# In the couples of the down projection the fifth block product is put ahead of the seventh, and the split of the third pair's gate weights is recorded in VectorE's fixed order

## The chip, the cores and the metric

The kernel runs on one core of a Trainium2 chip. The metric is the time of one execution on the device in microseconds, taken as the median of several runs. The kernel before took 1000.0 us (three runs: 999.8, 1000.0 and 1000.95).

## The reference

One layer of an encoder block on x of 1024 positions by 1024 channels, in float32. What matters here is its second half, the gated MLP, and the fact that everything is a chain of large matrix products:

```python
        y = jnp.concatenate([y_a, y_b], axis=-1)
        x = x + jnp.einsum("bse,ed->bsd", y, w_out[l])

        h = rmsnorm(x, norm_ffn_g[l])
        g = dwconv(jnp.einsum("bsd,df->bsf", h, w_gate[l]), conv_ffn_w[l])
        v = jnp.einsum("bsd,df->bsf", h, w_up[l])
        x = x + jnp.einsum("bsf,fd->bsd", jax.nn.silu(g) * v, w_down[l])

    return rmsnorm(x, norm_final_g)
```

`w_gate` and `w_up` are 1024 x 2816, `w_down` is 2816 x 1024. The first half (two mixing branches and `w_out`) is touched by nothing in this change.

## The kernel before, in words

**Precision.** Every float32 operand is split into a high part, rounded to the matmul's reduced format by a ScalarE copy (L131), and a low part, the difference, made by a VectorE or GpSimd subtraction (L93). A product of two such operands is three matmuls: high by high, high by low, low by high. In the profile `whi` and `wlo` are the parts of a weight, `r` is a part of an activation block or of a weight that lies in the same arena.

**Seven products instead of eight.** The MLP's matrices are taken two by two blocks at a time and multiplied by Strassen's scheme in Winograd's form. `class Pair` (L546 on) has the seven block products, each a method that issues its matmuls through `mul` (L557, so all of them carry that line) and then an `after...` method that takes the result out of PSUM:

- `m1` = A11 by B11, which opens bank `a`; `m6` = S2 by T2, `m7` = S3 by T3 and `m4` = A22 by T4 go on adding into the same bank `a`. After each of the four the bank is read once, so every next product into `a` waits until the reading after the last one is done.
- `m2` = A12 by B21 in a bank `b` of its own.
- `m5` = S1 by T1, which opens bank `c`; `m3` = S4 by B22 goes on in it.

A and S are weight blocks: A11 and A12 are split from the raw weights `raw`, A22 from the second raw weights `up` (split into `ahi` and `alo`). S1 and S2 are sums that GpSimd makes (L511, tile `s`) and that are then split by ScalarE and VectorE into `whi` and `wlo`; S3 and S4 are made later from the same tile `s` and, in the down projection, are split into the arena tile `r_99`. B and T are activation blocks.

**Gate and up.** For each of 22 column blocks `f`, gate and up are one `Ffn` pair of weights. Blocks 0 and 1 are multiplied without the scheme (`Plain`); blocks 2 to 21 with it. `g_job(f)` (L481) loads the gate weights of block `f` and splits them, `ff_prep(f)` (L728) calls it, then loads the up weights and makes the sums. The blocks 0 to 2 start in a section in which the order on TensorE and VectorE is fixed as recorded (`tc.manual_schedule(engines={nc.tensor.engine, V.engine})`); from block 3 on, in the loop that follows, only TensorE's order is fixed and a list scheduler places what the other engines do. The activations of the MLP go to DRAM as blocks B11, T2, B21, T3, T1, T4 and B22.

**Down.** `w_down` is multiplied in three chunks `ch` of six column blocks, plus a tail of four blocks without the scheme. A `Down` object is one pair of output row blocks; two of them make a couple, and there are six couples (0 to 5), two for each chunk. For each couple the loop at L950 records, on TensorE in this order: `m1` of both pairs; `m3` of the couple before; then the five steps of `STEPS` (L909), each for both pairs. One product is nine matmuls here, 18 for a couple. Inside this loop only TensorE's order is fixed. Around the products the scheduler places:

- the preparation of the next couple (`down_prep`): two loads of `raw` and `up` for each pair, the split of A11 and A12 (`wlo<-raw,whi`), the sums on GpSimd and their split (`wlo<-s,whi`), for which there are four pairs of buffers;
- `prep3`: the sums S3 and S4 and their split (`r_99<-s,r_99`), and the split of A22 (`alo<-up,ahi`);
- the readings. `after1` is a ScalarE copy and a GpSimd addition (L90). `after2`, `after4`, `after5` and `after3` are VectorE additions from PSUM into the output (L863, `xd<-xd,b` and the like). `after6` and `after7` are VectorE additions too, `xr<-xr,a`; only in couple 0 (`early`) they are a ScalarE copy (L542) and a GpSimd addition;
- in the second couple of a chunk, couples 1 and 3, the load of the next chunk's activation blocks (`load_op`, named in `STEPS` beside each product). A block is loaded once the product that read the old one is done, and each of its three parts is split on ScalarE and VectorE (`load_split`). B11, T2, B21, T3, T1, T4 and B22 lie one behind the other in the arena tiles `r_96`, `r_97`, `r_94`, `r_95`, `r_98` and `r_99`: T3 fills most of `r_94`, T1 most of `r_95`.

In the trace each engine takes its instructions in the order in which the program has them, and one that waits holds up those behind it on its engine.

The line that sets the order of the five steps is, before:

```python
    STEPS = (("m6", "T2"), ("m2", "B21"), ("m7", "T3"), ("m5", "T1"), ("m4", "T4"))
```

Of the kernel before, what the change touches and what calls it, by code (L numbers as in the profile page):

```python
# [27 lines left out]
NHEAD = 2  # L28
# [17 lines left out]
def block_kernel(ctx: ExitStack, tc, xT, win01, win, wout, wgate, wup, wdown, consts, outT):  # L46
# [75 lines left out]
    def hilo():  # L122
        return [wspl.tile([P, D], F32R, tag=t, name=t) for t in ("whi", "wlo")]

    def load_raw(p, tag, src, n=D):
        t = p.tile([P, n], F32, tag=tag, name=tag)
        nc.sync.dma_start(t, src)
        return t

    def split(y, hi, lo, lo_eng):  # L130
        nc.scalar.activation(hi, y, AF.Copy)  # L131
        minus(lo_eng, lo, y, f32(hi))
# [43 lines left out]
    def total_parts(a, eng):  # L176
        st = stp.tile([P, S], F32R, tag="st", name="st")
        hi, lo = st[:, :H], st[:, H:]
        nc.scalar.activation(hi, a, AF.Copy)
        minus(eng, lo, a, f32(hi))  # L180
        return hi, lo
# [299 lines left out]
    def g_job(f):  # L481
        raw = load_raw(wraw, "raw", wgate[f])
        hl = hilo()
        split(raw, *hl, nc.vector)
        return raw, hl
# [15 lines left out]
    def g_parts(hl, n):  # L501
        return {"A11": parts(hl, 0, n), "A12": parts(hl, n * P, n)}
# [222 lines left out]
    def raw_u(f):  # L725
        return load_raw(rup, "up", wup[f])

    def ff_prep(f):  # L728
        raw, hl = g_job(f)
        fp[f].w.update(g_parts(hl, 4))  # L730
        up, s = raw_u(f), Sums(4)
        fp[f].w.update(s.first(raw, up))
        fp[f].w.update(s.second(raw, up, a22p))
# [7 lines left out]
    with tc.manual_schedule(engines={nc.tensor.engine, V.engine}):  # L741
        with urgent():
            hl = total_parts(accs2[1], V)
# [41 lines left out]
        with urgent():  # L785
            to_op("T2", 0, 0)
        p2.w.update(s2.second(g2[0], up2))
        plain[1].second_b()
    ucp.release()

# [3 lines left out]
    with tc.manual_schedule(engines={nc.tensor.engine}):  # L794
        for p in plain:
            p.finish()
        for f in range(NHEAD, NF - 2):
            p, q = fp[f], fp[f + 1]
            ff_prep(f + 1)
            if f == NHEAD:  # L800
                p.m5()
                p.m6()
            else:
                p.m6()
                p.m5()
            q.m1()
            p.m7()
            q.m2()
            p.m4()
            p.m3()  # L810
# [5 lines left out]
    def xblock(o, k, z):  # L816
        return rblocks[OPS.index(o) * 2 * PPC + z * PPC + k]
# [5 lines left out]
    def load_op(ch, o):  # L823
        for k in range(PPC):
            load_split(xblock(o, k, 0), xblock(o, k, 1), yd[o][:, ch * PPC + k, :])
# [80 lines left out]
    def load_xd(d):  # L906
        nc.sync.dma_start(xf[d], x2d[d])

    STEPS = (("m6", "T2"), ("m2", "B21"), ("m7", "T3"), ("m5", "T1"), ("m4", "T4"))  # L909


    with tc.manual_schedule(engines={nc.tensor.engine}):
# [34 lines left out]
    with tc.manual_schedule(engines={nc.tensor.engine}):  # L947
        for d in range(3, KD):
            load_xd(d)
        for i, pair in enumerate(couples):  # L950
            ch = pair[0].ch
            reload = i % 2 and ch + 1 < NCH
            for p in pair:
                p.m1()
            if i:
                for p in couples[i - 1]:
                    p.m3()
            if reload:
                load_op(ch + 1, "B11")
            if ch and i % 2 == 0:  # L960
                load_op(ch, "B22")
            for p in pair:
                p.prep3()
            if i + 1 < len(couples):
                down_prep(i + 1)
            for step, o in STEPS:
                for p in pair:
                    getattr(p, step)()
                if reload:
                    load_op(ch + 1, o)  # L970


    free = rblocks[:16]
# [177 lines left out]
```

## Time and profile before

| what | value |
|---|---|
| median of three runs | 1000.0 us (999.8 to 1000.95) |
| the profiled execution | 1000.93 us |
| its span, first to last instruction | 999.1 us |
| mean granted TensorE clock | 0.993 |
| TensorE busy (4208 matmuls) | 967.5 us, 97% |
| VectorE busy (888 instructions) | 755.6 us, 76% |
| ScalarE busy (632) | 452.8 us, 45% |
| GpSimd busy (303) | 477.0 us, 48% |

The time of the profiled execution and its span differ by 1.8 us, which lies ahead of the first and behind the last instruction. The page of the profile lists busy time by engine and by group of instructions; the chain of waits follows the work that ended last back from the end; the timeline has instructions in order of time, with their start, their duration and, in brackets, the idle time of the engine just before them and who ended it. Engines are PE (TensorE), DVE (VectorE), ACT (ScalarE), POOL (GpSimd) and SP (the queue that issues loads and stores). A group such as `x18` is so many instructions one behind the other. The down section runs from about 759 to 934 us of the span, some 29 us for each couple.

### The profile page before, as it was taken

What the parts mean: (1) busy time and instruction counts of PE and PEld (TensorE: products, weight loads), DVE (VectorE), ACT (ScalarE), POOL (GpSimd) and SP (SyncE); (2) the same over time, 40 slices, a digit from 0 to 9 for tenths busy, and PEclk for the clock granted to TensorE, in tenths of its full rate; (3) what the DMA queues carried; (4) which work ended last, traced back from release to release, by engine and by line L of the source; (5) the groups of instructions that cost most, each with busy time, mean ns of one, the idle gap of its engine ahead of it and who ended that gap; (6) DMA issues with size and microseconds to landing.
All of it is one profiled execution on the core that took longest, in us unless ns stands there. A gap on an engine that the chain in (4) does not pass through costs nothing.

```text
span 999.1 us, 11602 instructions
## 1 busy us (share of the span) xinstructions
PE 967.5 (97%) x4208; PEld 790.8 (79%) x4208; DVE 755.6 (76%) x888; ACT 452.8 (45%) x632; POOL 477.0 (48%) x303
## 2 busy tenths in 40 slices
PE   7999999999999999999999999999998999999994
PEld 5788888888878887788888888888886787878883
DVE  7899999999578897855655565565569798796556
ACT  7454422234564456434444443444457263544353
POOL 4289754353853006554455456365336744352006
PEclk9999999999999999999999999999999999999998
DMA  6211111113554204143143133134284663643105
GB/s 257 85 44 63 43 45 61 42 64 106 193 190 153 76 0 158 64 148 106 64 145 108 64 124 129 64 101 141 70 287 130 220 207 96 194 127 109 61 1 169
DMA packets 63274, 112.56 MB, mean 113 GB/s; under 512 B 5488, under 2 KB 27120, under 8 KB 62960
## 3 DMA queue, kind: packets, MB, share of 16 engines
q1 hardware_dynamic: 62640, 110.65, 33.1%
q10 hardware_dynamic: 576, 1.17, 0.3%
q8 instruction: 33, 0.54, 0.2%
q14 instruction: 25, 0.20, 0.1%
HBM read 84.79 MB, written 27.00 MB: 112 GB/s over the span
## 4 chain that ended last, share of the span: by engine, by line
PE 81%; DVE 9%; ACT 3%; issue 2%; DMA 1%; POOL 1%; POOLq 0%; SPq 0%; DVEq 0%; ACTq 0%
PE a L557 30%; PE mm L166 20%; PE c L557 15%; PE b L557 7%; DVE r L93 2%; PE c L692 1%; PE a L692 1%; PE mm L153 1%; PE mm L152 1%; PE mm L154 1%; PE y L154 1%; PE y L152 1%; PE y L153 1%; DMA raw<-wgate 1%; ACT whi L131 1%
## 5 line engine op out<-in xcount | busy, mean ns | idle before, releaser
L166 PE MATMUL mm<-r,whi 128*128 128x512 f32 x576 | 155.8, 389 | 0.0
L557 PE MATMUL a<-r,whi 128*128 128x512 f32 x472 | 145.7, 390 | 0.4 <-ACT a L542 0.4
L323 DVE SCALAR_TENSOR_TENSOR cv<-u,cst,cv 128x512 f32<-128x512 f32 x203 | 138.9, 751 | 1.7 <-ACT cv L317 1.2
L511 POOL TENSOR_TENSOR s<-raw,s 128x512 f32<-128x512 f32 (+1 forms) x31 | 57.5, 1854 | 161.5 <-DVE wlo L93 161.5
L166 PEld LDWEIGHTS mm<-r,whi 128*128 128x128 f32 x576 | 108.1, 188 | 22.6
L557 PE MATMUL c<-r,whi 128*128 128x512 f32 x392 | 121.1, 390 | 0.0
L93 POOL TENSOR_TENSOR wlo<-raw,whi 128x1024 fp32r<-128x1024 f32 x30 | 77.5, 2586 | 88.0 <-ACT whi L131 88.0
L131 ACT ACTIVATE whi<-raw 128x1024 fp32r<-128x1024 f32 (+1 forms) x68 | 69.2, 1020 | 103.5 <-PE mm L166 32.0
L557 PEld LDWEIGHTS a<-r,whi 128*128 128x128 f32 x472 | 88.4, 188 | 19.7 <-ACT a L542 0.8
L511 POOL TENSOR_TENSOR s<-up 128x512 f32<-128x512 f32 (+1 forms) x31 | 42.0, 1354 | 116.7 <-DMA up<-wup 96.8
L557 PE MATMUL a<-r,wlo 128*128 128x512 f32 x236 | 92.2, 391 | 2.8 <-DVE wlo L93 2.8
L166 PE MATMUL mm<-r,wlo 128*128 128x512 f32 x288 | 90.0, 389 | 0.0
L557 PEld LDWEIGHTS c<-r,whi 128*128 128x128 f32 x392 | 73.8, 188 | 16.0
L542 ACT ACTIVATE a<-a 128x512 f32<-128x512 f32 x80 | 47.5, 595 | 66.9 <-PE a L557 64.2
L131 ACT ACTIVATE whi<-s 128x1024 fp32r<-128x1024 f32 (+1 forms) x52 | 52.5, 1010 | 53.5 <-PE c L557 39.8
L557 PE MATMUL c<-r,wlo 128*128 128x512 f32 x196 | 76.5, 390 | 0.0
L635 DVE TENSOR_TENSOR t<-a,c 128x512 f32<-128x512 f32 x40 | 27.5, 687 | 64.4 <-ACT a L542 38.1
L557 PE MATMUL a<-r,ahi 128*128 128x512 f32 x224 | 70.5, 396 | 1.4 <-ACT a L542 1.4
L557 PE MATMUL b<-r,whi 128*128 128x512 f32 x232 | 71.4, 389 | 0.0
L93 DVE TENSOR_TENSOR wlo<-s,whi 128x1024 fp32r<-128x1024 f32 (+1 forms) x52 | 64.2, 1236 | 5.8 <-ACT whi L131 5.7
L131 ACT ACTIVATE r<-r 128x512 fp32r<-128x512 f32 x71 | 43.8, 628 | 49.8 <-DMA r<-ydB 23.3
L166 PEld LDWEIGHTS mm<-r,wlo 128*128 128x128 f32 x288 | 54.1, 188 | 11.2
(214 smaller groups left out, 2142.0 us busy)
## 6 DMA issues: line engine op xcount, KB each, us to landing
raw<-wgate SPq DMA_DIRECT2D x22, 512.0 KB, 4.9
up<-wup SPq DMA_DIRECT2D x20, 512.0 KB, 3.6
raw<-win SPq DMA_DIRECT2D x18, 512.0 KB, 3.2
ydT<-t SPq DMA_DIRECT2D x36, 256.0 KB, 3.4
r<-ydT SPq DMA_DIRECT2D x36, 256.0 KB, 3.3
raw<-wout SPq DMA_DIRECT2D x16, 512.0 KB, 3.4
ydB<-t SPq DMA_DIRECT2D x27, 256.0 KB, 5.0
r<-ydB SPq DMA_DIRECT2D x27, 256.0 KB, 4.5
```

Source lines behind the costliest of these rows:

```text
L93: eng.tensor_tensor(out=out, in0=a, in1=b, op=ALU.subtract)
L131: nc.scalar.activation(hi, y, AF.Copy)
L152: nc.tensor.matmul(out, whi, hi, start=first, stop=False)
L153: nc.tensor.matmul(out, whi, lo, start=False, stop=False)
L154: nc.tensor.matmul(out, wlo, hi, start=False, stop=last)
L166: nc.tensor.matmul(outs[h], w, a[h][z], start=s0, stop=s1)
L323: nc.vector.scalar_tensor_tensor(fin if k == KC - 1 else acc, src, w, acc, ALU.mult, ALU.add)
L511: self.eng.tensor_tensor(out=self.t[:, i * self.w : (i + 1) * self.w], in0=a, in1=b, op=op)
L542: nc.scalar.activation(t, b, AF.Copy)
L557: nc.tensor.matmul(out, w[wz][:, k, :], x[xz], start=first and k + wz + xz == 0, stop=k == n - 1 and wz == 1, skip_group_check=not first)
L635: nc.vector.tensor_tensor(out=out, in0=a, in1=b, op=op)
L692: nc.tensor.matmul(out, w[wz][:, k, :], xz, start=first and k == 0 and wz == 0 and xz is hi, stop=not first and k == 3 and wz == 1)
```

## The change

It has two parts.

The first swaps two of the five steps of a couple. `m5` now comes before `m7`, and both loads that hung on `m7` and `m5`, T3 and T1, are recorded after `m7`:

```diff
-    STEPS = (("m6", "T2"), ("m2", "B21"), ("m7", "T3"), ("m5", "T1"), ("m4", "T4"))
+    STEPS = (("m6", ("T2",)), ("m2", ("B21",)), ("m5", ()), ("m7", ("T3", "T1")), ("m4", ("T4",)))
...
-            for step, o in STEPS:
+            for step, ops in STEPS:
                 for p in pair:
                     getattr(p, step)()
                 if reload:
-                    load_op(ch + 1, o)
+                    for o in ops:
+                        load_op(ch + 1, o)
```

The second takes the load and split of block 3's gate weights out of the loop and records it in the section before, in which VectorE's order is fixed, ahead of the last products of block 1:

```diff
-    def ff_prep(f):
-        raw, hl = g_job(f)
+    def ff_prep(f, job=None):
+        raw, hl = job or g_job(f)
...
         p2.w.update(s2.second(g2[0], up2))
+        job = g_job(NHEAD + 1)
         plain[1].second_b()
...
-            ff_prep(f + 1)
+            ff_prep(f + 1, job if f == NHEAD else None)
```

What this does to the order of the instructions, engine by engine: on all five engines the instructions, and what each waits for, are the same in both kernels from the start up to the middle of couple 0. The second part thus changes numbers of buffers, and moves nothing. On TensorE, in each of the six couples the 18 matmuls of `m5` now stand ahead of the 18 of `m7`; at the end, couple 5's `m4` stands some matmuls later among those of the tail.

VectorE in couple 1, before. The names ending in 5700 and 5701 are the outputs of the couple's two pairs; `a` is read after `m7`, `c` after `m5`; `r_94` and `r_97` are splits of reloaded blocks, `wlo<-s` is the split of S1 and S2 for couple 2:

```order
L93 TENSOR_TENSOR r_94<-r_94,r_97 128x512
L863 TENSOR_TENSOR xr_5700<-xr_5700,a 128x512
L93 TENSOR_TENSOR r_94<-r_94,r_97 128x512
L863 TENSOR_TENSOR xr_5701<-xr_5701,a 128x512
L93 TENSOR_TENSOR r_94<-r_94 128x512 x2
L863 TENSOR_TENSOR xr_5700<-xr_5700,c 128x512
L93 TENSOR_TENSOR wlo<-s,whi 128x768
L93 TENSOR_TENSOR r_94<-r_94 128x512
L863 TENSOR_TENSOR xr_5701<-xr_5701,c 128x512
L93 TENSOR_TENSOR wlo<-s,whi 128x768
```

The same place in the changed kernel, from the same split of `r_94` on:

```order
L93 TENSOR_TENSOR r_94<-r_94,r_97 128x512
L864 TENSOR_TENSOR xr_5700<-xr_5700,c 128x512
L93 TENSOR_TENSOR wlo<-s,whi 128x768
L93 TENSOR_TENSOR r_94<-r_94,r_97 128x512
L864 TENSOR_TENSOR xr_5701<-xr_5701,c 128x512
L93 TENSOR_TENSOR wlo<-s,whi 128x768
L93 TENSOR_TENSOR r_95<-r_95 128x512 x2
L864 TENSOR_TENSOR xr_5700<-xr_5700,a 128x512
L93 TENSOR_TENSOR r_95<-r_95 128x512
L864 TENSOR_TENSOR xr_5701<-xr_5701,a 128x512
L93 TENSOR_TENSOR r_94<-r_94 128x512 x3
```

The addition after `m7` of the couple's first pair (`xr_5700<-xr_5700,a`) now stands behind both additions of `c`, both splits of the next couple's sums and two splits of T1. Between the addition that comes before it on bank `a` (after `m6` of the second pair) and itself stood ten instructions; now there are seventeen: those ten and two additions of `c`, two splits `wlo<-s`, one more split of `r_94` and two of `r_95`. Couple 3 has the same seven.

ScalarE in couple 0, before. `a_5840` and `a_5852` are the copies of bank `a` after `m7` of the two pairs, `whi<-s` is the high part of couple 1's S1 and S2, `t` belongs to the last gate/up blocks:

```order
L131 ACTIVATE whi<-raw 128x768 x2
L542 ACTIVATE a_5840<-a 128x512
L613 ACTIVATE t<-t 128x1024
L542 ACTIVATE a_5852<-a 128x512
L131 ACTIVATE whi<-s 128x768 x2
L131 ACTIVATE ahi<-up 128x384 x2
```

And after, where the same two copies are called `a_5862` and `a_5874`:

```order
L131 ACTIVATE whi<-raw 128x768 x2
L131 ACTIVATE whi<-s 128x768
L613 ACTIVATE t<-t 128x1024
L131 ACTIVATE whi<-s 128x768
L542 ACTIVATE a_5862<-a 128x512
L542 ACTIVATE a_5874<-a 128x512
L131 ACTIVATE ahi<-up 128x384 x2
```

Both copies of bank `a` have moved behind both copies of the sums.

SP in couple 0, before. `xd_5699`, `xr_5700` and `xr_5701` are the output rows to which the products are added, `raw` and `up` are weights of couple 2:

```order
L616 DMA ytail<-t 128x1024 x2
L907 DMA xd_5699<-x2d 128x1024
L907 DMA xr_5700<-x2d 128x1024 x2
L907 DMA xr_5701<-x2d 128x1024 x2
L831 DMA raw<-wdown 128x3x128 x2
L831 DMA up<-wdown 128x3x128
```

And after:

```order
L616 DMA ytail<-t 128x1024 x2
L832 DMA raw<-wdown 128x3x128 x2
L908 DMA xd_5699<-x2d 128x1024
L908 DMA xr_5700<-x2d 128x1024 x2
L908 DMA xr_5701<-x2d 128x1024 x2
L832 DMA raw<-wdown 128x3x128 x2
```

Two loads of couple 2's raw weights, which wait until GpSimd has made couple 1's last sum from the same buffer, now stand ahead of the loads of the output rows.

## The prediction

> **What bounds the kernel now.** I read the page first. These lines are the span, TensorE's busy time and the shares of the chain of work that ended last:
>
> ```profile
> span 999.1 us, 11602 instructions
> PE 967.5 (97%) x4208; PEld 790.8 (79%) x4208; DVE 755.6 (76%) x888; ACT 452.8 (45%) x632; POOL 477.0 (48%) x303
> ...
> PE 81%; DVE 9%; ACT 3%; issue 2%; DMA 1%; POOL 1%; POOLq 0%; SPq 0%; DVEq 0%; ACTq 0%
> ```
>
> TensorE is busy for nearly the whole span and is 81% of the chain. So the kernel gets faster only where TensorE stands still, and slower where it is made to. The view of TensorE's waits names who was late, among others these (total us, times, longest):
>
> ```profile
> PE a L557 <- DVE r L93: 3.4, 2, 2.8
> ...
> PE a L557 <- DVE xd L863: 1.9, 2, 1.4
> ```
>
> Both concern products into bank `a`, which is where the change works. The chain of waits in order of time shows what a product costs in the down section. Its columns are start, duration, engine and line, count:
>
> ```profile
> 800.32 4.08 PE b L557 x18
> 804.40 4.08 PE a L557 x18
> 808.48 4.08 PE c L557 x18
> 812.56 8.31 PE a L557 x36
> ...
> 829.03 4.09 PE b L557 x18
> ...
> 834.52 4.35 PE a L557 x18
> ...
> 871.65 8.31 PE a L557 x36
> ...
> 888.12 2.05 PE b L557 x9
> ...
> 892.64 4.34 PE a L557 x18
> ```
>
> A product of a couple is 18 matmuls in 4.08 us, 0.227 us each. Couple 1 runs without a hole: second product at 800.32, seventh at 804.40, fifth at 808.48, fourth at 812.56. The x36 rows are the fourth product and the next couple's first. The other rows are the holes. In couple 2 the second product ends at 829.03 + 4.09 = 833.12, and the seventh starts at 834.52 and takes 4.35 instead of 4.08: 1.67 us lost. In couple 4 the second product has nine matmuls from 888.12 to 890.17, and nine more would end at 892.21; the seventh starts at 892.64 and takes 4.34: 0.69 lost. The large hole is in couple 0; these are TensorE's rows of its seventh product, up to the fifth:
>
> ```profile
> 769.98 0.61 PE L557 MATMUL a<-r,r 128*128 128x512 f32 x2
> 771.23 2.33 PE L557 MATMUL a<-r,r 128*128 128x512 f32 x9 [0.64 <-DVE r L93]
> 776.33 3.35 PE L557 MATMUL a<-r,r 128*128 128x512 f32 x7 [2.76 <-DVE r L93]
> 779.48 0.71 PE L557 MATMUL c<-r,whi 128*128 128x512 f32 x2
> ```
>
> The 18 matmuls take from 769.98 to 779.48, that is 9.50 us for work of 4.08: 5.42 lost. It waits for VectorE's splits of the sums S3, one for each pair:
>
> ```profile
> 769.13 2.05 DVE L93 TENSOR_TENSOR r<-s,r 128x768 fp32r<-128x768 f32 x1
> ...
> 774.26 2.01 DVE L93 TENSOR_TENSOR r<-s,r 128x768 fp32r<-128x768 f32 x1
> ```
>
> The seven matmuls from 776.33 to 779.48 are 3.15 us for work of 7 x 0.227 = 1.59, so 1.56 of the 5.42 is no wait but a slower clock. The view by windows shows that (width, busy times of PE, PEld, DVE, ACT and POOL, granted clock, DMA share and rate):
>
> ```profile
> 772.80:776.20 3.40, 0.77 (x4) 0.30 (x2) 3.40 (x3) 0.60 (x1) 3.40 (x3) 1.00 0.33 131
> 776.20:779.60 3.40, 3.27 (x8) 2.60 (x9) 3.40 (x4) 1.06 (x1) 3.32 (x3) 0.50 0.08 30
> ```
>
> **The second part of the change** moves no instruction, so TensorE's wait for that split, in the gate/up section, stays, and the part costs and brings nothing. The first row has the wait, the second what follows it; had the split moved, at most 1.8 us could go:
>
> ```profile
> 382.08 0.50 PE L557 MATMUL a<-r,wlo 128*128 128x512 f32 x1 [1.79 <-DVE wlo L93]
> 382.42 0.63 PE L557 MATMUL a<-r,whi 128*128 128x512 f32 x2
> ```
>
> **What the first part takes away.** With the fifth product in front, TensorE has 4.08 us of work from 769.98 to 774.06 that needs no S3. S1 and T1 are there: S1 is split together with S2, which the sixth product has already used, and T1's splits in couple 0 end long before. Then the first pair's seventh product needs the split that ended at 771.18, and the second pair's third matmul, due at 774.06 + 2.04 + 2 x 0.227 = 776.6, the one that ended at 776.27. The whole 5.42 goes. In couples 2 and 4 the wait is for the reading of bank `a` after the sixth product, late by less than 4.08, so it goes too. Together: 5.42 + 1.67 + 0.69 = 7.78 us.
>
> **What it brings: the fourth product comes straight behind the seventh.** Before, the fifth stood between them and gave the readers of bank `a` 4.08 us more. Now the first pair's fourth product is due when the second pair's seventh ends, 2.04 us after the first pair's. Who reads the bank, and what stands ahead of that reading, decides.
>
> Couple 0: the readers are ScalarE copies. Before, they ran when the seventh product was done. ScalarE's rows from the second of them on:
>
> ```profile
> 779.72 0.60 ACT L542 ACTIVATE a<-a 128x512 f32<-128x512 f32 x1 [0.35 <-PE a L557]
> 781.67 0.85 ACT L131 ACTIVATE whi<-s 128x768 fp32r<-128x768 f32 x1 [1.35 <-PE c L557]
> ```
>
> Now both copies stand behind both `whi<-s`, and the second of these needs GpSimd's sum of couple 1's second pair, in which nothing changes up to its end:
>
> ```profile
> 779.17 1.61 POOL L511 TENSOR_TENSOR s<-s,raw 128x384 f32<-128x384 f32 x1
> ```
>
> That sum ends at 780.78. The split's high part (0.85) then ends at about 781.7, and the copy (0.60) at 782.2. The seventh product ends at 778.14, so TensorE stands still for about 4.1 us. If GpSimd were a microsecond earlier it would be 3.1; 4.3 is the other end. Before, the fourth product started at 779.48 + 4.08 = 783.6, so couple 0 starts it only 1.3 earlier for all that was taken away.
>
> Couple 1: the reader is a VectorE addition, in a queue with no gaps. VectorE's rows, from the addition after the sixth product to the one after the seventh, and some behind it:
>
> ```profile
> 803.74 0.67 DVE L863 TENSOR_TENSOR xr<-xr,a 128x512 f32<-128x512 f32 x1
> 804.34 0.68 DVE L93 TENSOR_TENSOR r<-r 128x512 fp32r<-128x512 f32 x1
> 804.94 1.28 DVE L93 TENSOR_TENSOR r<-r,r 128x512 fp32r<-128x512 f32 x2
> ...
> 810.89 0.67 DVE L863 TENSOR_TENSOR xr<-xr,a 128x512 f32<-128x512 f32 x1
> ...
> 814.49 0.95 DVE L93 TENSOR_TENSOR wlo<-s,whi 128x768 fp32r<-128x768 f32 x1
> ...
> 816.55 1.18 DVE L93 TENSOR_TENSOR wlo<-s,whi 128x768 fp32r<-128x768 f32 x1
> 817.66 2.93 DVE L93 TENSOR_TENSOR r<-r 128x512 fp32r<-128x512 f32 x2
> ```
>
> From 804.34 to 810.89 lie ten instructions, eight of 512 columns at a step of 0.60 (804.34 to 804.94) and two of 768 columns, which leaves 0.87 for each. Now seven more stand ahead: two additions of `c`, one split of `r_94`, two of `r_95` (5 x 0.60) and two `wlo<-s` (2 x 0.87), 4.74 in all. The addition starts at 815.63 and ends at 816.30. The fourth product is due at 812.56 in either order, so it waits 3.7 us at the least. More is likely, since GpSimd makes its second sums as soon as the first `wlo<-s` is done:
>
> ```profile
> 815.51 1.40 POOL L511 TENSOR_TENSOR s<-raw,s 128x384 f32<-128x384 f32 x1 [12.24 <-DVE wlo L93]
> ...
> 820.00 1.47 POOL L511 TENSOR_TENSOR s<-raw,up 128x384 f32<-128x384 f32 x1
> ```
>
> They run for 6.0 us (815.51 to 821.47), and under them the second `wlo<-s` took 1.18 instead of 0.95 and two splits of `r_95` took 2.93 instead of 1.28. Before, that lay behind the addition. Now the first `wlo<-s` is the twelfth behind 804.34 and ends at about 804.34 + 9 x 0.60 + 3 x 0.87 = 812.4, so the sums fall on what lies ahead of the addition: 0.23 + 1.65 = 1.88 more, and the wait is 5.6 us. With the split of `r_94` slowed as well (0.8) it is 6.4. I take 5.6, since these are the same instructions under the same sums.
>
> Couple 3 has the same seven extra instructions:
>
> ```profile
> 860.40 1.27 DVE L863 TENSOR_TENSOR xr<-xr,a 128x512 f32<-128x512 f32 x2
> 861.60 2.71 DVE L93 TENSOR_TENSOR r<-r,r 128x512 fp32r<-128x512 f32 x2
> ...
> 868.97 0.68 DVE L863 TENSOR_TENSOR xr<-xr,a 128x512 f32<-128x512 f32 x1
> ```
>
> The addition goes from 868.97 to 873.71 and ends at 874.39; the fourth product is due at 871.65: 2.7 us, or 4.6 with GpSimd. Here two splits had already been slowed before (2.71 at 861.60), so not all is new. I take 3.6. Couples 2, 4 and 5 reload nothing: their queue holds only additions and the next splits, and the addition follows in time. I cost them at nothing; without that cover it would be some tenths each.
>
> The clock: one gap of 2.76 us cost 1.56 behind it, while behind the gap of 1.79 us at 382 two matmuls took 0.63, as two took 0.61 at 769.98, so the clock stayed full there. All three new gaps are longer than 2.76. I take the full 1.56 for the longest, and 1.0 for each of the others, since work may resume in the middle of a slow stretch: 3.6, with ends 0 and 4.7. The Trainium skill's "TensorE: Matmul & The Clock Gate", section "What's actually happening", says that the array falls to half rate only after a whole idle window of some 3.4 us, and that the windows run freely. By that rule a gap of 3.6 would hardly ever count and the longer ones only by luck of phase, so by it this term would be nearer to 1.5 and the sum 2 us less; the trace disagrees, with half rate behind 2.76 us.
>
> **What costs nothing else.** T1's reload starts 4 us earlier and T3's 4 us later, by the ends of their products, and each is needed only in the next couple's fifth or seventh, over 20 us on. The bank `c` opens 4 us earlier; its last user, two products of the couple before, is done by then. On SP two loads of raw weights now stand ahead of the output rows, and this addition waited for such a row already:
>
> ```profile
> 789.37 0.69 DVE L863 TENSOR_TENSOR xd<-xd,a 128x512 f32<-128x512 f32 x1 [1.91 <-DMA xd<-x2d]
> ```
>
> If the row comes 4 us later, the addition ends at 794. It is now the one after the fifth product, and the third product of that pair is due at about 794 as well. I take 0, with 1.0 as the upper end.
>
> **The sum.** -7.8 + 4.1 + 5.6 + 3.6 + 3.6 = +9.1 us. The profiled execution took 1000.93 (its span of 999.1 and 1.8 around it), so it would become 1010.0; it lies 0.9 above the median of the three runs, 1000.0, and on the median the forecast is 1009.1. The lower ends give -7.8 + 3.1 + 3.7 + 2.7 + 0 = +1.7, the upper ones -7.8 + 4.3 + 6.4 + 4.6 + 4.7 + 1.0 = +13.2.
>
> **The rivals.**
>
> *VectorE is in time (faster).* The place is the addition after the first pair's seventh product in couples 1 and 3. It turns where that addition ends before the fourth product is due, 812.56 in couple 1: seventeen instructions of 11.3 us and 0.67 must then start at 800.6, straight behind the sixth product, and not at 804.34. What speaks for it: in couple 3 the addition after the sixth product already came at 860.40, under 1 us behind the product (three products before 871.65 is 859.4). Against it: even there the new addition is 2.7 late. Only couple 0's gap and its clock would be left: -7.8 + 4.1 + 1.0 = -2.7, or 997.3.
>
> *The clock stays at full rate.* All three gaps come, and none is followed by a slow stretch: 9.1 - 3.6 = +5.5, 1005.5. For it speaks that the gap of 1.79 us left the clock alone; against it the 2.76. The Trainium skill's clock rule, above, is on this side.
>
> *Short queues.* GpSimd's sums fall elsewhere and the clock stays: -7.8 + 4.1 + 3.7 + 2.7 = +2.7, 1002.7.
>
> *Lateness is passed on.* The output rows hold up a third product and the queue in couples 2 and 4 is still late: 13.2 and some 2 more, 1015. Against it: each new gap of TensorE gives VectorE time to catch up.
>
> *The second part does what it says.* The wait of 1.8 us at 382 goes: 1007.3. The order speaks against it on every engine.
>
> **How the numbers follow.** Forecast, 1009.1 with a range of its own from 1006 to 1013.5: 0.68. Clock at full rate, 1005.5: 0.14. Short queues, 1002.7: 0.06. Passed on, 1015: 0.06. In time, 997.3: 0.05. Second part, 1007.3: 0.01. The range from 1003 to 1014 leaves out the short queues, the passed-on lateness and the rival in time, 0.17. A measurement of this kernel can tell 0.2%, or 2 us, from no change: below 998 lies the rival in time, 0.05; between 998 and 1002 the lower half of the short queues and what lies near, 0.04; above, 0.91.
>
> **What would show it.** In the profile after: TensorE's seventh product of couple 0 without a wait for VectorE's `r`, some 5 us gone; its fourth product in couple 0 waiting for ScalarE's copy (L542) for about 4 us, in couples 1 and 3 for VectorE's `xr` for about 5.6 and 3.6; the two holes in couples 2 and 4 gone; granted clock 0.50 behind the new gaps; the wait at 382 unchanged. I am wrong if the fourth product follows the seventh without a gap in couple 1, or if VectorE's addition there ends before 813.

## The result and the profile after

The changed kernel takes 1015.62 us (median of 4 runs, 1014.05 to 1016.75), the kernel before beside it 999.9 (999.42 to 1000.95): a ratio of 1.0155, 95% interval 1.0137 to 1.0172, 15.7 us slower. The forecast was 1009.1 with a range up to 1014.0. The sign and the places were as forecast, the size was not.

The profiled execution took 1016.0 us. Its span, TensorE's busy time and the shares of the chain of waits, from the page of the profile after:

```profile
span 1014.2 us, 11602 instructions
PE 972.8 (96%) x4208; PEld 795.6 (78%) x4208; DVE 754.4 (74%) x888; ACT 452.9 (45%) x632; POOL 473.0 (47%) x303
...
PE 74%; DVE 8%; issue 4%; ACT 4%; DMA 4%; POOL 3%; SPq 0%; POOLq 0%; ACTq 0%; DVEq 0%
```

The instructions are the same. TensorE's share of the chain fell from 81% to 74%, and DMA's rose from 1 to 4. TensorE's waits in the down section (758 to 940), total us, times and longest:

```profile
PE a L557 <- DVE xr L864: 11.5, 2, 7.4
PE a L557 <- ACT a L542: 4.1, 2, 3.9
PE a L557 <- DVE wlo L93: 0.7, 1, 0.7
```

The two waits of before, for VectorE's `r` and `xd`, are gone. In their place the fourth product waits for the readers of bank `a`. TensorE's rows in couples 0, 1 and 3, the seventh product (x18) and the first of the fourth:

```profile
773.65 4.24 PE L557 MATMUL a<-r,r 128*128 128x512 f32 x18
781.76 1.22 PE L557 MATMUL a<-r,ahi 128*128 128x512 f32 x2 [3.87 <-ACT a L542]
...
809.23 4.24 PE L557 MATMUL a<-r,r 128*128 128x512 f32 x18
820.89 1.22 PE L557 MATMUL a<-r,ahi 128*128 128x512 f32 x2 [7.42 <-DVE xr L864]
...
876.34 4.24 PE L557 MATMUL a<-r,r 128*128 128x512 f32 x18
884.62 1.22 PE L557 MATMUL a<-r,ahi 128*128 128x512 f32 x2 [4.04 <-DVE xr L864]
```

All three seventh products run through in 4.24 us, couple 0's too. From the start of the eighteenth matmul (0.227 us before the due time) to the next one it is 4.03, 7.58 and 4.20 us more than a step. And the clock behind each gap, by windows (width, busy times of PE, PEld, DVE, ACT and POOL, granted clock, DMA share and rate):

```profile
777.60:781.00 3.40, 0.29 (x2) 0.00 (x0) 3.40 (x4) 1.70 (x3) 2.67 (x2) 1.00 0.00 0
781.00:787.80 6.80, 6.04 (x14) 4.83 (x15) 6.24 (x7) 1.72 (x4) 5.09 (x4) 0.50 0.22 83
...
818.60:825.40 6.80, 4.51 (x11) 3.54 (x12) 5.71 (x9) 1.15 (x2) 2.50 (x2) 0.50 0.51 154
...
883.40:890.20 6.80, 5.58 (x13) 4.42 (x14) 5.63 (x9) 1.79 (x3) 1.43 (x2) 0.50 0.65 187
```

Before, one slow stretch of 3.4 us lay in this section. Now there are three of 6.8. In couple 0's fourth product three matmuls take 1.28 us at clock 0.50 (782.78 to 784.06) and 0.69 at full rate (788.11 to 788.80), so 0.46 of what lies between the first matmul and the end of the stretch is lost: 0.46 x (787.8 - 781.76) = 2.8 in couple 0, 0.46 x (825.4 - 820.89) = 2.1 in couple 1, 0.46 x (890.2 - 884.62) = 2.6 in couple 3, 7.4 together with the parts unrounded. With it the difference of the spans, 15.1 us, is told within 0.4 us: 4.03 + 7.58 + 4.20 + 7.4 - 7.78 = 15.4.

Where a kernel was run beside the kernel before on another chip, that took 1000.5 to 1000.8 there, and the ratios below are to it. They are worked out from the single runs, so they can differ a little from the quotient of the two medians.

### The profile page after: what moved, and what is told of

Read it like the earlier page. It is cut to its first block, busy times and chain, and to the rows that moved or that the text cites. A ratio compares the mean times of both kernels' runs of the same rounds, so it can differ in the third digit from the quotient of the medians.

```text
span 1014.2 us, 11602 instructions
## 1 busy us (share of the span) xinstructions
PE 972.8 (96%) x4208; PEld 795.6 (78%) x4208; DVE 754.4 (74%) x888; ACT 452.9 (45%) x632; POOL 473.0 (47%) x303
## 4 chain that ended last, share of the span: by engine, by line
PE 74%; DVE 8%; issue 4%; ACT 4%; DMA 4%; POOL 3%; SPq 0%; POOLq 0%; ACTq 0%; DVEq 0%
PE a L557 27%; PE mm L166 19%; PE c L557 13%; PE b L557 6%; DVE r L93 2%; POOL s L511 2%; PE c L692 1%; PE a L692 1%; DMA raw<-wout 1%; PE y L154 1%; PE y L152 1%; PE y L153 1%; ACT whi L131 1%; ACT r L131 1%; DMA r<-ydT 1%
## 5 line engine op out<-in xcount | busy, mean ns | idle before, releaser
L557 PE MATMUL a<-r,ahi 128*128 128x512 f32 x224 | 76.5, 425 | 16.0 <-DVE xr L864 11.5
L557 PEld LDWEIGHTS a<-r,ahi 128*128 128x128 f32 x224 | 45.6, 205 | 28.3 <-DVE xr L864 12.3
```

Source lines behind the costliest of these rows:

```text
L557: nc.tensor.matmul(out, w[wz][:, k, :], x[xz], start=first and k + wz + xz == 0, stop=k == n - 1 and wz == 1, skip_group_check=not first)
```

## Experiments: the parts one by one

The changed kernel with the new order of the steps in some couples alone (`i in (0,)`, `(1, 3)`, `(2, 4, 5)`), and one with the second part alone:

```diff
-            for step, ops in STEPS:
+            for step, ops in STEPS if i in (0,) else OLD:
```

> The changed kernel with the new order of the steps in couple 0 alone; the other five couples keep the old order. Theory (each couple adds its own part: in couple 0 the hole of 5.4 us ahead of the seventh product goes, a wait of 4.0 us ahead of the fourth product comes, and about 3.2 us of slow clock behind it): +1.8 us, 1001.7. Rival (my prediction's size of the clock term, 1.0 in this couple): -5.4 + 4.0 + 1.0 = -0.4, 999.5. Second rival (the lateness of couple 0 is what delays couple 1, in either order of couple 1): over 1003, with a wait in couple 1.

> The new order in couples 1 and 3 alone. Theory (nearly all of the loss is here: waits of 7.6 and 4.2 us ahead of the fourth product and 2.2 and 2.6 us of slow clock behind them): +16.6, 1016.5. If 1.2 us of couple 1's wait were inherited from couple 0, whose moved loads let the first splits of the reloaded block come late, couple 1's wait is 6.4 here, and the time 1015.3. Rival (my prediction: 5.6 and 3.6 us, clock 1.56 and 1.0): +11.8, 1011.7.

> The new order in couples 2, 4 and 5 alone, where nothing is reloaded. Theory (the holes of 1.67 and 0.69 us in couples 2 and 4 go, and the fourth product's wait stays covered): -2.4, 997.5. Rival (these queues are late as well as soon as couples 1 and 3 do not hold TensorE up): a wait ahead of the fourth product of some tenths to 2 us with slow clock behind it, 999 to 1002.

> Only the second part of the change: the split of block 3's gate weights recorded in the section with VectorE's fixed order, all couples in the old order. Theory (it moves no instruction): 999.9, and the wait of 1.8 us at 382 stays. Rival (it lets the split come in time): 998.1 without that wait.

| kernel | median us | ratio to before, 95% | difference by the ratio, us | forecast for this part |
|---|---|---|---|---|
| couple 0 | 1003.39 | 1.0026 (1.0015 to 1.0038) | +2.6 | -5.4 + 4.1 + 1.0 = -0.3 |
| couples 1 and 3 | 1014.04 | 1.0134 (1.0115 to 1.0153) | +13.4 | 5.6 + 3.6 + 2.6 = +11.8 |
| couples 2, 4 and 5 | 1000.93 | 1.0003 (0.9989 to 1.0017) | +0.3 | -2.4 |
| second part | 999.80 | 0.9997 (0.9986 to 1.0007) | -0.3 | 0 |

The four sum to 16.0, the whole has 15.5 by its ratio. Each of the first three came out 1.6 to 2.9 above its forecast, so no single term was wrong alone. That they add up so nearly is in part chance, since the parts act on each other, as the rows below show. The second part does nothing, as forecast.

Two rows say more. With the new order in couples 1 and 3 alone, couple 1 waits only 4.7 us, not 7.4:

```profile
818.67 1.22 PE L557 MATMUL a<-r,ahi 128*128 128x512 f32 x2 [4.68 <-DVE xr L864]
```

The rest of its wait is thus inherited from couple 0. Counted as above, couples 1 and 3 wait 4.8 and 4.6 us here, 9.4 together where the prediction had 9.2; the slow clock behind them takes 4.8 where it had 2.6. With the new order in couples 2, 4 and 5 alone, the hole of couple 2 only moves, from the seventh to the fourth product:

```profile
836.07 4.24 PE L557 MATMUL a<-r,r 128*128 128x512 f32 x18
842.47 0.73 PE L557 MATMUL a<-r,ahi 128*128 128x512 f32 x2 [2.16 <-DVE xd L864]
```

VectorE is still behind from couple 1's reload. In the whole change this wait does not come, because couple 1 has already held TensorE up for 7.4 us. The kernel with couples 1 and 3 alone bears that out: there too couple 2 has no wait for `xd`, although it keeps the old order.

## Experiments: the clock

To keep TensorE busy in the gaps without touching the waits, extra products go into a bank that nobody reads, in the changed kernel and in the one with couples 1 and 3:

```diff
+                if step == "m7" and i in FILL:
+                    z = bank2("z")
+                    for j in range(FILL[i]):
+                        pair[0].mul(z, "A22", "T4")
```

> The changed kernel with extra products in the three gaps: behind the seventh products of couples 0, 1 and 3 TensorE multiplies A22 by T4 into a bank that nobody reads, 18, 27 and 18 matmuls (4.1, 6.1 and 4.1 us at full rate), so that it is not idle while it waits for the readers of bank a. The waits themselves stay, covered by this work. Theory (the three slow stretches of 6.83 us come from the idle time ahead of them, and cost about 8.0 us together): 1015.6 - 8.0 = 1007.6, no clock of 0.50 in the down section; up to 1.5 less if the loads of couple 2's weights come earlier here and shorten couple 1's wait. My prediction's size of the clock term (3.6): 1012. Rival (the slow stretches do not come from idleness): 1015 or more, with 0.50 in the same places.

> The kernel with the new order in couples 1 and 3 alone (1014.0 us), with 18 extra matmuls (4.1 us, A22 by T4 into a bank that nobody reads) behind the seventh product of each of the two, where its waits of 4.8 and 4.6 us were followed by slow stretches. Theory (the slow clock comes from idleness, and here it lies on the path): no clock of 0.50 behind these two places and 2.45 + 2.7 = 5.1 us less, 1008.9. Rival (what TensorE wins by it, it loses at the next reading, since VectorE's queue and not TensorE sets the time here): no slow stretches either, but 1013 to 1014, with other waits longer by as much. Rival (the stretches do not come from idleness): 1014 with the 0.50 there.

The second (`FILL = {1: 2, 3: 2}`) took 1009.93 us, ratio 1.0094 (1.0079 to 1.0109), where the same order without the extra work has 1.0134 (1.0115 to 1.0153): 4.0 us less, of 5.1 expected. The clock by windows from the start of the fourth product in couples 1 and 3:

```profile
817.40:824.20 6.80, 6.80 (x30) 5.53 (x31) 5.80 (x10) 2.81 (x5) 0.17 (x1) 1.00 0.70 201
880.10:886.90 6.80, 6.80 (x30) 5.53 (x31) 5.96 (x11) 3.53 (x7) 0.06 (x1) 1.00 0.78 227
```

Thirty matmuls fit into 6.8 us, where the slow stretches of the change held eleven and thirteen and a rest of the gap. So the slow stretches come from the idle time, and in these two couples they are on the path.

The first (`{0: 2, 1: 3, 3: 2}`) took 1014.86, ratio 1.0140 (1.0120 to 1.0159), hardly less than the changed kernel: its expectation of 1007.6 failed. The slow stretches of couples 0 and 3 are gone, couple 1's of 6.8 us stays, and the time is not won. The chain of waits in order of time shows why:

```profile
786.90 0.38 SPq L832
...
787.87 5.93 DMA xd<-x2d
793.83 0.70 DVE xd L864
...
794.57 2.33 PE c L557 x9
```

Couple 0's third product now waits for the addition that read bank `c`, this for an output row, and that row stood on SP behind a load of raw weights. What couple 0 wins, it loses 10 us later at a row: its third product is due at 790.73 instead of 792.91, but the product behind it, couple 1's sixth, starts at 796.74, against 796.99 in the change. This is the move on SP that the prediction had priced at nothing. And what couple 3 wins by its clock is lost in couple 1, whose fourth product starts at 822.92 instead of 820.89, after a wait of 3.4 us: there the up weights had waited 3.9 us on SP for VectorE's split `alo` of the weights before them.

## Experiments: couple 1's wait

Four DMAs of couple 2's raw weights go to GpSimd's queue, where they stand behind GpSimd's own sum and hold up no load on SP; in another kernel the output rows go to ScalarE's queue; in a third GpSimd's second sums for couples 2 and 4 are left out:

```diff
-            nc.sync.dma_start(
+            (nc.gpsimd if tag == "raw" and ch == 1 and d < 4 else nc.sync).dma_start(
...
-        nc.sync.dma_start(xf[d], x2d[d])
+        nc.scalar.dma_start(xf[d], x2d[d])
...
+            if sums:
                 self.op(1, g[:, w : 2 * w], self.t[:, w : 2 * w], ALU.subtract)
                 self.op(0, g[:, :w], v[:, :w], ALU.subtract)
```

> The changed kernel with the loads of couple 2's raw weights, four DMAs, issued by GpSimd's queue instead of SP's. On SP the output rows then follow the last stores of the tail at once, as before the change, and the up weights and the first reload follow them. Theory (the two raw loads that wait on SP for GpSimd's sum make the up weights and the reload late, and that is the part of couple 1's wait that is gone where couple 0 keeps the old order, 7.6 against 4.8): couple 1's wait falls to about 4.8, the time to 1012.9. Rival (these loads are late for another reason, or do not matter): wait of 7 or more, 1015.6.

> The changed kernel with the output rows that stood behind two loads of raw weights on SP issued by ScalarE's queue instead, so that the loads of couple 2's up weights and the first reload of couple 1 come earlier on SP. Theory (couple 1's wait of 7.6 holds about 2.5 us that come from SP's queue in couple 0: first sums of GpSimd 4 us late, and with them the splits of the reloaded block): that wait falls to about 5, the time by 2 to 2.7, to 1013.2. Rival (couple 1's wait is as long as its own queue makes it): unchanged, 1015.6.

> The changed kernel without GpSimd's second sums (S3 and S4) for couples 2 and 4, the eight sums that run while VectorE works off the queue ahead of the addition in couples 1 and 3; their splits take the tile as it is. Theory (the sums slow the splits ahead of the addition by 1.8 us in each of the two couples): waits of about 5.8 and 2.4 instead of 7.6 and 4.2, with the slow clock behind them 1015.6 - 3.6 = 1012; one split of T1 also falls behind the addition in both couples, 0.6 each, so 1010.8. Rival (only the number of instructions ahead of the addition counts): just these 1.2, 1014.4.

The raw loads off SP: 1012.25 us, ratio 1.0118 (1.0103 to 1.0134), about 3.7 us less than the change. Couple 1 waits as long as without couple 0's change (counted as above 4.6 us, 2.9 less than in the change; the rest is, in this profile, a shorter slow clock):

```profile
817.64 1.22 PE L557 MATMUL a<-r,ahi 128*128 128x512 f32 x2 [4.49 <-DVE xr L864]
```

What lies between is seen in VectorE's rows of the changed kernel, from the first splits of the reloaded block to the addition, and in the DMA issues between 795 and 808 (KB each, median us from issue to landing):

```profile
803.09 0.89 DVE L93 TENSOR_TENSOR r<-r 128x512 fp32r<-128x512 f32 x1 [3.08 <-ACT r L131]
804.81 0.69 DVE L93 TENSOR_TENSOR r<-r 128x512 fp32r<-128x512 f32 x1 [0.83 <-ACT r L131]
805.42 0.68 DVE L864 TENSOR_TENSOR xr<-xr,a 128x512 f32<-128x512 f32 x1
806.04 0.89 DVE L93 TENSOR_TENSOR r<-r 128x512 fp32r<-128x512 f32 x1
806.85 1.51 DVE L93 TENSOR_TENSOR r<-r,r 128x512 fp32r<-128x512 f32 x1
...
816.29 1.15 DVE L93 TENSOR_TENSOR wlo<-s,whi 128x768 fp32r<-128x768 f32 x1
817.37 2.88 DVE L93 TENSOR_TENSOR r<-r 128x512 fp32r<-128x512 f32 x2
820.16 0.67 DVE L864 TENSOR_TENSOR xr<-xr,a 128x512 f32<-128x512 f32 x1
```

```profile
r<-ydT SPq DMA_DIRECT2D x4, 256.0 KB, 6.1
up<-wdown SPq DMA_DIRECT2D x3, 192.0 KB, 6.2
```

With the old order in couple 0 (the kernel with couples 1 and 3 alone) the same places read:

```profile
801.34 2.98 DVE L93 TENSOR_TENSOR r<-r 128x512 fp32r<-128x512 f32 x2 [0.90 <-ACT r L131]
804.24 0.68 DVE L864 TENSOR_TENSOR xr<-xr,a 128x512 f32<-128x512 f32 x1
```

```profile
r<-ydT SPq DMA_DIRECT2D x3, 256.0 KB, 3.1
up<-wdown SPq DMA_DIRECT2D x1, 192.0 KB, 5.0
```

In the change the up weights come later and run beside the reload. T2's block (`ydT`) lands in 6.1 us instead of 3.1. B11's (`ydB`), the first, lands in 6.1 instead of 4.9, and the last two of its three loads are issued 2.0 and 2.4 us later, at 798.31 and 799.26. So VectorE's splits start late, at 803.09. GpSimd's first sums, late as well, run mostly beside the splits behind the addition at 805.42, which take 0.81 and 1.43 by their starts for 0.60, and not beside those ahead of it. The seventeen instructions ahead of the addition of bank `a` were counted rightly. Against the fourth product's due time (809.23 + 4.08 = 813.31) the queue begins 7.9 us ahead, where in the profile of before it was 812.56 - 803.74 = 8.8; and it takes 14.1 us (806.04 to 820.16) and not the 11.3 + 1.9 = 13.2 of the prediction. The two differences, 0.9 and 1.0, make up the 1.9 to 2.0 us by which the wait is longer than 5.6.

The rows on ScalarE's queue: 1013.36, ratio 1.0131 (1.0110 to 1.0152), an interval that overlaps that of the change. The time is near the 1013.2 expected, but not by the way expected: couple 1 waits 7.3 us in the profile, not 5, and the span of that execution, 1014.3, is as long as the change's. It decides nothing: the four issues of rows took until 796.3 on ScalarE's queue, and SP's loads still came late, three of the four up weights at 797 or after.

Without the second sums: 1009.92, ratio 1.0087 (1.0067 to 1.0108). Couples 1 and 3 wait 4.3 and 2.4 us instead of 7.4 and 4.0. VectorE's rows in couple 1 at the place of 816.29 above:

```profile
816.62 0.95 DVE L93 TENSOR_TENSOR wlo<-s,whi 128x768 fp32r<-128x768 f32 x1
817.49 0.68 DVE L93 TENSOR_TENSOR r<-r 128x512 fp32r<-128x512 f32 x1
818.09 0.68 DVE L865 TENSOR_TENSOR xr<-xr,a 128x512 f32<-128x512 f32 x1
```

One split of T1 stands ahead of the addition instead of two, and it takes 0.68 where the pair took 2.88. From the start of `wlo<-s` to that of the addition it is 1.47 us instead of 3.87; 0.60 of the difference is the missing split, 1.80 are GpSimd's sums. So these do slow VectorE here, by the size that the prediction had read from the trace of before (1.88).

## Experiments: couple 0, and a search for a faster version

In couple 0 alone, two other orders of fifth and seventh product, so that one or both of ScalarE's copies of bank `a` stand ahead of the split that waits for GpSimd:

```diff
+            if i == 0:
+                for step, e in (("m6", 0), ("m6", 1), ("m2", 0), ("m2", 1), ("m5", 0), ("m7", 0), ("m5", 1), ("m7", 1), ("m4", 0), ("m4", 1)):
+                    getattr(pair[e], step)()
+                continue
```

> Couples 1 to 5 in the old order; in couple 0 fifth and seventh product alternate by pairs: fifth and seventh of the first pair, fifth and seventh of the second, then the fourth of both. The copy of the first pair's bank a then stands ahead of the second split of the sums on ScalarE, the copy of the second pair's bank still behind it. Theory (the wait of 4.0 us ahead of the fourth product comes from ScalarE's copies standing behind that split, which waits for GpSimd): the first pair's copy ends at about 779.5 and the wait is 1.6 us, the second pair's about 0.7 more, no or one slow stretch: -5.4 + 2.3 + 0 to 1.7, against 1000.5 for the kernel before 997.4 to 999.1. Rival (the copy is late by the seventh product itself or by the activation ahead of it, whatever stands behind): a wait of 3 to 4 us as with the new order in couple 0 alone, 1002 to 1003.

> Couples 1 to 5 in the old order; in couple 0 the first pair's fifth product ahead of both seventh products and the second pair's behind them. Both copies of bank a stand ahead of the second split on ScalarE. Theory: no wait ahead of the fourth product, but one of 2.2 us within the second pair's seventh, for its S3, with one or two slow stretches of 1.7 us each behind it: -5.4 + 2.2 + 1.7 to 3.4, 999.0 to 1000.7. Rival (the fourth product waits as long as with the new order, so that it is not the place of the copies): 1002 or more.

Both did to the fourth product what was expected, and neither to the time: 1003.55, ratio 1.0026 (1.0014 to 1.0037), and 1003.77, 1.0031 (1.0019 to 1.0043), as with the change itself in couple 0 (1.0026). The pairwise order, TensorE's fourth product, VectorE's addition of bank `c`, and TensorE's wait for it:

```profile
780.60 0.73 PE L557 MATMUL a<-r,ahi 128*128 128x512 f32 x2 [1.59 <-ACT a L542]
```

```profile
795.28 0.69 DVE L864 TENSOR_TENSOR xd<-xd,c 128x512 f32<-128x512 f32 x1 [5.03 <-DMA xd<-x2d]
```

```profile
PE c L557 <- DVE xd L864: 4.6, 1, 4.6
```

The copies' place does set the fourth product's wait: 3.9 us with both behind, 1.6 with one, none with both ahead. But three patterns of waits give one time. In the two new ones the third product waits for the row, 4.6 and 5.4 us; in the order of the change it does not, since its fourth product is late by 4 us already.

With the raw loads on GpSimd's queue besides, and that queue alone in the kernel before as a control:

> c0_pairwise with couple 2's raw weights loaded by GpSimd's queue, so that the output rows come first on SP. Theory (in couple 0 not only the reading of bank a but the output row for the addition of bank c sets the end: what the order of the products wins is lost at the third product as long as the row is late): the third product's wait of 4.8 us and its slow stretches go, 1.8 us ahead of the fourth product stay: 1000.6 - 5.4 + 1.8 + 0 to 1.7 = 997.0 to 998.7. Rival (the row is late by the traffic, not by SP's order): 1003.5 again.

> c0_m5_between with the same change of queue. Theory: the third product's wait of 5.6 us and its slow stretches go; the gap of 1.8 us within the seventh product stays: 1000.6 - 5.4 + 1.8 + 0 to 1.7 = 997.0 to 998.7. Rival: 1003.7 again.

> The kernel before with couple 2's raw weights loaded by GpSimd's queue, and nothing else. Theory (there the output rows stand ahead of these loads on SP already, so the queue wins nothing by itself): 1000.6, within 1. Rival (loads on GpSimd's queue are worth something whatever the order of the products, so that the two runs beside this one show that and not the row): 998 or less.

The rows then land earlier; in the pairwise order the addition waits 1 us for its row:

```profile
790.88 0.69 DVE L864 TENSOR_TENSOR xd<-xd,c 128x512 f32<-128x512 f32 x1 [0.99 <-DMA xd<-x2d]
```

and the third product waits 0.6 us instead of 4.6. So the row was late by SP's order, not by traffic. The time did not follow: 1002.91, ratio 1.0032 (1.0019 to 1.0044). The waits moved on, into couples 1 and 2:

```profile
PE a L557 <- DVE xd L864: 3.0, 1, 3.0
PE a L557 <- ACT whi L131: 1.7, 1, 1.7
```

With the fifth product of the second pair behind, 1001.43, ratio 1.0011 (1.0002 to 1.0020): the third product still waits 3.3 us, since VectorE's addition waits for one of GpSimd's, which stands behind the issue of the raw loads. The control gave 1000.67, ratio 1.0004 (0.9995 to 1.0013): nothing by itself, as expected.

Three versions joined what had worked, with the next couple's first product ahead of the fourth:

```diff
+                if step == "m4" and i + 1 < len(couples):
+                    for p in couples[i + 1]:
+                        p.m1()
```

> An attempt at a faster version: the new order in couples 0, 2, 4 and 5, the old one in 1 and 3, and in every couple the next couple's first product recorded ahead of the fourth, so that 4.1 us more lie between the seventh and the fourth product. Theory (a hole goes only if 4 us or more of work that needs neither S3 nor bank a stand on both sides of the seventh product): no holes in couples 0 and 2 (5.4 and about 2 us) and none new: against 1000.8 for the kernel before on the same chip 993.3. Rival (the queue of VectorE is what is late, and an earlier first product moves the reloads and the holes along): holes of 1 to 4 us in other places, 996 to 1003.

> The mixed version again (new order in couples 0, 2, 4, 5, old in 1 and 3, the next couple's first product ahead of the fourth), with couple 2's raw weights loaded by GpSimd's queue, so that the output rows come earlier on SP. Theory (what held the mixed version up was one wait of 3.4 us, couple 0's third product for the addition of bank c, which waits for an output row; with the row at about 790 it goes, and its 3 us of slow clock too): 6 us less than the mixed version, 995.5. Rival (the row is late by DMA traffic and not by SP's order): 1001.7.

> As the version before it, with couple 0's third product moved behind couple 1's sixth, so that the addition it waits for has 4 us more. Theory: as that version or up to 1 us better, 994.5 to 995.5, since the wait is gone with some reserve. Rival (couple 1's sixth product then stands 4 us earlier and waits for the split of its sums, which end at about 787, or VectorE's queue moves on bank a): 997 to 1002.

They took 1001.68, ratio 1.0013 (1.0003 to 1.0022); 999.60, 0.9993 (0.9983 to 1.0003); and 1000.37, 1.0000 (0.9991 to 1.0010). In the last, couple 0's third product stands behind the split of couple 1's S4 into the same tile, so it multiplies another weight. All three expectations of 993 to 995.5 failed, and none is faster than the kernel before by what can be told. In the first, the third product waits for the row (3.2 us). In the second that is 0.6, and what was won comes back in small waits, none over 1.2:

```profile
PE a L557 <- DVE xd L864: 2.0, 3, 1.2
PE a L557 <- DVE wlo L93: 1.9, 2, 1.2
PE c L557 <- DVE xd L864: 0.6, 1, 0.6
```

Which transfer or engine sets the pace of couples 0 to 2 as a whole was not settled.

## Why the prediction was right in sign and too small

In the profiled execution the terms come to 15.4 us where the sum had 9.1. Of the 6.3 missing, 3.8 are the clock, 2.0 couple 1's wait and 0.6 couple 3's. Neither the clock nor couple 1's wait alone would have carried the time out of the range. Point by point, by its steps:

- *The second part moves nothing*: right, 0.9997 (0.9986 to 1.0007).
- *The holes that go, 7.78 us*: right in the profile, all three are gone. But the sum took them as won. Couples 2, 4 and 5 alone win nothing (+0.3), since couple 2's hole moves to the fourth product; it goes in the whole change only because couple 1's longer wait lets VectorE catch up. And 1.56 of couple 0's 5.42 was clock, which differs from execution to execution: behind the same hole of 2.7 to 2.8 us no slow stretch follows in the profiles of the second part alone and of couples 2, 4 and 5 alone, one in that of before, and two in those of couples 1 and 3 alone and of the control with GpSimd's queue.
- *Couple 0's wait, 4.1*: right in size (4.03) and cause; the place of ScalarE's copies sets it.
- *Couple 1's wait, 5.6*: too small, 7.6. The instructions and GpSimd's part were right. What failed is the step "On SP two loads of raw weights now stand ahead of the output rows ... I take 0, with 1.0 as the upper end". It looked at one addition only. Behind the rows on the same queue stand the up weights and couple 1's reload; they came late and met, and VectorE's queue began 0.9 us later and took 1.0 longer. Taking those loads off SP brought couple 1's wait down to 4.5 and won 3.7 us of the time.
- *The whole of couple 0*: forecast -0.3, measured +2.6. In the profile of couple 0 alone the miss is the clock, 2.8 for 1.0 (slow from the fourth product at 783.08 to 789.19), and couple 2's hole, 2.1 us of wait for 1.4. But the step on SP stands right behind: three orders of its products with waits of 4, 1.6 and 0 us ahead of the fourth gave the same time. Where the fourth product is not late, the row is.
- *Couple 3's wait, 3.6*: nearly right, 4.2, within its bounds.
- *The clock, 3.6 (0 to 4.7)*: too small, 7.4 by the trace. The price of 1.56 came from the one gap of before, after which work resumed at 776.33, just behind the edge of a slow stretch at 776.2. The three new gaps reach 0.8, 2.3 and 1.2 us into a slow stretch, and the next stretch was slow as well, so each gap has two. The bound "the full 1.56" was no upper end but near the lowest: over all profiles the gaps of 3.7 us and more have 3.4 to 6.1 us of slow clock behind them, 1.6 to 2.8 us of loss. In couples 1 and 3, 4.0 us of clock were shown to be on the path (forecast there: 2.6). In couple 0 the clock's 2.8 was in the chain of the changed kernel, but taking it away won nothing, because the row was next.
- *The gap at 382 costs no clock*: wrong as a rule. In the profile after, the same wait of 1.8 us is followed by a slow stretch:

```profile
381.79 0.79 PE L557 MATMUL a<-r,wlo 128*128 128x512 f32 x1 [1.81 <-DVE wlo L93]
...
410.97 0.73 PE L557 MATMUL a<-r,ahi 128*128 128x512 f32 x2 [0.63 <-ACT a L542]
```

```profile
411.25 0.73 PE L557 MATMUL a<-r,ahi 128*128 128x512 f32 x2 [1.43 <-ACT a L542]
```

The second fence is the row of before. There no slow stretch follows at 382, and the wait at 411 is 0.8 us longer. What the slow clock takes, this later wait gives back in part, and by 411 all of it is back: the change is 0.29 us ahead of before at 382 and 0.28 at 411. So it cost the section nothing.

Of the rivals, "lateness is passed on" (1015, 0.06) comes nearest: output rows behind the raw loads, and a queue that is late. In the changed kernel itself the row does not show as a wait of the third product, since couple 0 is late anyway. The late queue shows some 25 us on, in couple 1, and not in couples 2 and 4, where that rival had it. So its time is met by other places than its own, which is luck. "The clock stays at full rate", "short queues" and "VectorE is in time" fell: every new gap was there, over its lower bound, with a slow stretch behind it.

So the steps that failed are two costs that were bounded too tightly: a queue's move by a single follower, and the clock by a single gap.

## What to carry to other kernels

When loads move on a queue, price every instruction behind them on that queue up to the next idle time, also two stages on, and not the one consumer that already waited. A hole ahead of one product is won only if the next reading, row or split has slack behind it: here three different orders of one couple gave the same time to 0.4 us. For the clock, a little under half of the time from the first matmul after a gap to the end of the slow stretches was lost: 2.1 to 2.8 us behind the three new gaps. One gap says little: behind the hole of 2.8 us in the old order it was nothing, 1.5 or 2.8 us in different executions, by where the grid of the stretches lay.

## What the runs showed of the hardware

The slow stretches lie on a fixed grid of 3.41 us, the same from the start to the end of an execution; its edges differ from run to run. In the change they begin at 381.64, 781.00, 818.55 and 883.40, which lie 117, 11 and 19 steps of 3.413 us apart. The rule for the fall was read over the gaps of all 19 profiles of this study, from the first record of the clock on. The idle time is counted from the end of the last matmul's row to the start of the next, and the edges are those of the granted clock. Where TensorE stood still for 1.95 us or more of the 3.41 of one stretch, the next was always at 0.50; at 1.6 or less of a stretch at full rate never. Between 1.65 and 1.93 it went either way: with the second part alone, 1.80 us in the stretch ahead of 382 were followed by a slow one, and 1.86 us in that from 771.4 were not. The wait of 1.8 us ahead of 382 lies just there, by phase with more or less of it in one stretch, and a slow stretch follows it in 11 of the 19 profiles. Once at 0.50, a stretch with 0.62 us or more of idle time at its start was followed by another at 0.50 in all 17 cases, and one with 0.31 or less never. The Trainium skill's "TensorE: Matmul & The Clock Gate", section "What's actually happening", has free-running windows of 3413 ns, half rate after at least one idle window and full rate after a busy one. The grid and the return agree; for the fall, 1.95 us of 3.41 were enough here, not a whole window.
